# Stick-breaking attention: its softplus written as max(a, 0) + ln(1 + exp(-|a|)), with the absolute value on ScalarE

## The chip, the cores and the metric

The kernel runs on one core of a Trainium2 chip. A core has five engines that run at the same time, each through its own queue in order: TensorE (matrix products, PE in the profile), VectorE (DVE), ScalarE (ACT, functions of one input), GpSimd (POOL) and SyncE (SP, which here issues DMA transfers). They wait for each other only through semaphores. The metric is the device time of one execution in microseconds (us); lower is better. Of the kernel before three runs are known, and one more execution was profiled.

## The reference

One decoder block over 1024 tokens of width 1024: a state-space branch and an attention branch side by side, merged by gates, then a feed-forward network (FFN). The change concerns the attention branch, which has 8 heads of width 64 and weighs keys by stick breaking:

```python
z = jnp.einsum('bhqd,bhkd->bhqk', qb, kh) * scale
mask = key_pos < q_pos
log_not = jnp.where(mask, jax.nn.log_sigmoid(-z), 0.0)
suffix = lax.cumsum(log_not, axis=3, reverse=True) - log_not
weights = jnp.where(mask, jnp.exp(jax.nn.log_sigmoid(z) + suffix), 0.0)
return jnp.einsum('bhqk,bhkd->bhqd', weights, vh)
```

With softplus s(z) = ln(1 + exp(z)), `log_sigmoid(-z)` is -s(z) and `log_sigmoid(z)` is z - s(z). So a weight is the exponential of z minus the sum of s over this key and all later ones that the query sees, and s is needed once for each score.

## The kernel before

All products are f32 accurate: an operand is split into a high part in a reduced format and a low part (what is left), and three products of these parts are added. TensorE therefore issues three matmuls where one would do, and VectorE, ScalarE and GpSimd do the splits. The program runs through projections and the state-space branch, attention, the merge of the branches, the output projection, and the FFN.

**Attention** works on 40 units. A unit holds scores of two heads (one pair of heads shares the 128 partitions of q and k) for one or two blocks of 128 keys against up to 512 queries, with the keys on the partitions: a tile of 128 x 2 x w. For each of the 4 head pairs there are 10 units, 3 for the first 512 queries and 7 for the others, with the keys from the last to the first. Six of the 10 lie on the diagonal and take a mask; four of these are narrow (2 x 384), all other units are 2 x 512. The last four units of a pair have no mask.

A unit goes through three functions, and the loop in `attention` overlaps three units:

- `scores` (three units ahead): TensorE writes the scores into `z`, of which there is one PSUM buffer. They are copied to `a` (tile `wa`), with the mask added on VectorE (L871) or by a plain copy on ScalarE (L873). Then the softplus in tile `ws`: GpSimd takes min(a, 40) (L874), ScalarE Exp (L875) and Ln(1 + x) (L876), and VectorE max(a, that) (L877), which restores large values that the bound cut off. VectorE then splits it into `wh` (L878) and `wl` (L879). There are five buffers of `wa` and two each of `ws`, `wh` and `wl`.
- `sums`: TensorE multiplies the parts with a triangle of ones and adds the carried row of the units before, into `acc`, of which there is one PSUM buffer. ScalarE copies the total as the next carried row (L900), VectorE subtracts `acc` from `a` in two halves (L902) and takes the low part of the row (L904), and ScalarE applies the exponential (L905).
- `values`: TensorE multiplies the weights with V.

Between these, `fillers` gives TensorE matmuls of projections that are needed later (8 at each of two places in a unit), so that it has work while a unit's chain runs on the other engines. Their weights are split by L454, L456 and L457 on ScalarE, VectorE and GpSimd, and their results leave by copies (L841, L843, L846).

The matmuls of attention stay in the order in which the code issues them. The other engines' order is chosen when the program is built, by a scheduler with a model of the durations; each engine's list is then fixed. A change of durations or engines can therefore move instructions elsewhere too, as far as the first products of the FFN (`seven`, L1247), whose operands are formed and split on ScalarE and VectorE (L473, L475, L476).

The `acc` buffer sets the tightest loop: TensorE may start the next unit's sums only when L900, L902 and L904 have read it.

Of the kernel before, what the change touches and what calls it, by code (L numbers as in the profile page):

```python
# [12 lines left out]
AF = mybir.ActivationFunctionType  # L13
ALU = mybir.AluOpType
# [346 lines left out]
P = 128  # L361
KT = 8
MASKED = -1.0e30
EXACT = 40.0

AK, ARB = 1, 2

# [60 lines left out]
class Block:  # L428
# [421 lines left out]
    def scores(self, u, qk, work):  # L850


        nc = self.nc
        q, k = qk[u.hp]
        u.a, s = (work.tile([P, 2, 512], F32, name=t, bufs=b) for t, b in (("wa", WAB2), ("ws", WSB)))
        u.parts = [work.tile([P, 2, 512], F32R, name=t, bufs=WHB) for t in ("wh", "wl")]
        z = self.zp.tile([P, 2, 512], F32, name="z")
        u.segs, f, diag = [], 0, u.kbs[0] >= 4 * u.Q
        for kb in u.kbs:
            c = max(kb - 4 * u.Q, 0) * P  # L860
            w = 512 - c
            for x in range(2):
                h = slice(64 * x, 64 * x + 64)
                self.pinned(z[:, x, f:f + w], lhsT=k[h, P * kb:P * kb + P], rhs=q[h, 512 * u.Q + c:512 * u.Q + 512], start=True, stop=True)
            u.segs.append((kb, slice(f, f + w), slice(c, 512)))
            f += w
        u.f = f
        a, st, ht, lt, z = (t[:, :, 0:f] for t in (u.a, s, *u.parts, z))
        if diag:
            m = P * (2 - len(u.kbs))  # L870
            nc.vector.tensor_tensor(a, z, self.mask[:, m:m + f].unsqueeze(1).broadcast_to([P, 2, f]), ALU.add)  # L871
        else:
            nc.scalar.copy(a, z)  # L873
        nc.gpsimd.tensor_scalar(st, a, EXACT, None, ALU.min)  # L874
        nc.scalar.activation(st, st, AF.Exp)  # L875
        nc.scalar.activation(st, st, AF.Ln, bias=1.0)  # L876
        nc.vector.tensor_tensor(st, a, st, ALU.max)  # L877
        nc.vector.tensor_scalar(ht, st, 1.0, 0.0, ALU.mult, ALU.add)  # L878
        nc.vector.tensor_tensor(lt, st, ht.bitcast(F32), ALU.subtract)  # L879

# [650 lines left out]
```

## Time and profile before

| | |
|---|---|
| median of 3 runs | 1520.55 us (1516.18 to 1520.73) |
| profiled execution | 1517.3 us, of which the span of the profile 1515.5 |
| mean granted TensorE clock | 0.973 |

Busy time of the engines by stage, in us, from the windows of the profile:

| stage | span | length | TensorE | VectorE | ScalarE | GpSimd |
|---|---|---|---|---|---|---|
| projections, state-space branch, gates | 0 to 380 | 380 | 339.6 | 265.1 | 111.3 | 23.9 |
| attention | 380 to 677 | 297 | 289.1 | 247.6 | 171.9 | 145.0 |
| merge of the branches | 677 to 740 | 63 | 54.5 | 48.8 | 29.1 | 24.7 |
| output projection | 740 to 860 | 120 | 114.5 | 62.8 | 48.5 | 13.1 |
| FFN, gate and up | 860 to 1190 | 330 | 326.2 | 218.7 | 107.2 | 153.3 |
| FFN, down, last norm | 1190 to 1515 | 325 | 298.4 | 291.3 | 115.5 | 251.6 |

In the rows that follow, `L874` is line 874 of the kernel before; a group's row reads: line, engine, operation, tile written <- tiles read, shapes, count | busy us, mean ns of one | us that the engine sat idle before them, and what ended that. A row of the timeline reads: start us, duration us, engine, line, operation, tiles, shapes, count, and in brackets idle time before it. A window's row gives for each engine busy us and the number of instructions, then the granted clock, the share of the DMA engines and GB/s. A busy TensorE is not one at its peak, since matmuls overlap in the record.

### The profile page before, as it was taken

How to read it: one execution, taken by the hardware profiler on the slowest of the kernel's cores; microseconds unless marked ns; L12 is line 12 of the kernel's file. 1: busy time of each engine (PE TensorE's matmuls, PEld its weight loads, DVE VectorE, ACT ScalarE, POOL GpSimd, SP SyncE). 2: the span in 40 equal slices, each digit the busy share in tenths (PEclk: the TensorE clock that was granted, in tenths of full speed). 3: DMA queues.
4: the chain of work that ended last, by engine and by line, in shares of the span. 5: the costliest groups of instructions: out<-in, count | busy, mean ns of one | idle time of the engine just before them, and what ended most of it. 6: DMA issues, size and time to landing. Idle time of an engine off the chain costs nothing.

```text
span 1515.5 us, 18316 instructions
## 1 busy us (share of the span) xinstructions
PE 1422.3 (94%) x6706; PEld 1121.7 (74%) x6706; DVE 1134.3 (75%) x1523; ACT 583.5 (38%) x764; POOL 611.6 (40%) x306
## 2 busy tenths in 40 slices
PE   5898999997999999999799799999999998999995
PEld 3678888786666666658688588888888886888774
DVE  5779985455887988877625886666666769999998
ACT  3321122622474656564317533333333224343323
POOL 1000000102455555424300145444444468788795
PEclk9999999999999999999999899999999999999998
DMA  9555665388111112117523233333333246445312
GB/s 341 139 112 165 160 160 151 123 283 285 42 42 42 36 49 77 49 57 249 178 87 112 84 111 125 105 104 104 105 105 104 87 152 240 147 160 171 106 51 111
DMA packets 180410, 193.55 MB, mean 128 GB/s; under 512 B 28636, under 2 KB 130080, under 8 KB 180320
## 3 DMA queue, kind: packets, MB, share of 16 engines
q1 hardware_dynamic: 171184, 184.86, 38.8%
q10 hardware_dynamic: 8912, 7.48, 1.8%
q8 instruction: 53, 0.87, 0.2%
q14 instruction: 37, 0.30, 0.1%
q0 software_dynamic: 224, 0.05, 0.0%
HBM read 142.40 MB, written 48.76 MB: 126 GB/s over the span
## 4 chain that ended last, share of the span: by engine, by line
PE 40%; DVE 23%; issue 12%; DMA 10%; POOL 9%; ACT 5%; SPq 1%; DVEq 0%; POOLq 0%; ACTq 0%
PE tq L1247 10%; PE wo L1247 8%; PE wo L1128 5%; POOL ws L874 3%; DMA aw<-in_w_ada_dram 3%; PE gu L1247 3%; PE mm L809 2%; PE mm L643 2%; PE mx L809 2%; PE ga L735 1%; PE acc L809 1%; DVE acc L979 1%; POOL pb L1307 1%; PE mx L735 1%; DVE wa L902 1%
## 5 line engine op out<-in xcount | busy, mean ns | idle before, releaser
L874 POOL TENSOR_SCALAR ws<-wa 128x1024 f32<-128x1024 f32 (+1 forms) x40 | 109.3, 2733 | 117.6 <-DVE wa L871 59.0
L473 POOL TENSOR_TENSOR ws<-wb 128x1024 f32<-128x1024 f32 x26 | 64.2, 2471 | 191.1 <-DMA wb<-in_w_ffn_up_dram 88.6
L457 POOL TENSOR_TENSOR wl<-ws,wh 128x1024 fp32r<-128x1024 f32 x12 | 29.1, 2421 | 122.5 <-ACT wh L454 76.5
L294 POOL MEMSET tz<- 128x1024 f32 x4 | 3.8, 954 | 178.0 <-PE mm L643 95.2
L877 DVE TENSOR_TENSOR ws<-wa,ws 128x1024 f32<-128x1024 f32 (+1 forms) x40 | 46.8, 1169 | 35.6 <-ACT ws L876 35.2
L1300 POOL TENSOR_TENSOR pa<-pa,row 128x1024 f32<-128x1024 f32 x22 | 66.2, 3032 | 0.7 <-DMA pa<-in_w_ffn_down_dram 0.7
L875 ACT ACTIVATE ws<-ws 128x1024 f32<-128x1024 f32 (+1 forms) x40 | 38.9, 972 | 69.3 <-POOL ws L874 69.3
L473 POOL TENSOR_TENSOR wgs<-wb 128x1024 f32<-128x1024 f32 x14 | 35.6, 2540 | 73.3 <-DVE wgl L476 31.1
L1238 POOL TENSOR_TENSOR f<-f,f 128x512 f32<-128x512 f32 x30 | 49.0, 1660 | 26.1 <-DVE f L1228 17.6
L879 DVE TENSOR_TENSOR wl<-ws,wh 128x1024 fp32r<-128x1024 f32 (+1 forms) x40 | 55.6, 1390 | 1.1
L979 DVE SCALAR_TENSOR_TENSOR acc<-aw,cond,acc 128x512 f32<-128x512 f32 x56 | 44.0, 786 | 9.3 <-DMA aw<-in_w_ada_dram 8.5
L809 PE MATMUL z<-q,k 64*128 64x512 f32 (+3 forms) x192 | 42.6, 535 | 6.9 <-DVE gst L1062 6.9
L902 DVE TENSOR_TENSOR wa<-wa,acc 128x512 f32<-128x512 f32 (+1 forms) x80 | 46.7, 624 | 2.7 <-PE acc L809 1.8
L454 ACT CAST wh<-ws 128x1024 fp32r<-128x1024 f32 x24 | 25.0, 1048 | 59.7 <-PE wo L1128 34.9
L1227 ACT ACTIVATE f<-f 128x1024 f32<-128x1024 f32 x22 | 23.3, 1061 | 58.7 <-DVE f L1267 31.3
L1329 POOL TENSOR_TENSOR wb<-pa 128x512 f32<-128x512 f32 x23 | 39.6, 1731 | 15.6 <-DVE wxl L1327 5.5
L905 ACT ACTIVATE wa<-wa 128x1024 f32<-128x1024 f32 (+1 forms) x40 | 38.6, 964 | 13.8 <-DVE wa L902 13.8
L1238 POOL TENSOR_TENSOR f<-f 128x512 f32<-128x512 f32 x20 | 42.2, 2128 | 0.0
L1346 PE MATMUL wo<-f,f 128*128 128x512 f32 x132 | 40.6, 389 | 0.0
L476 DVE TENSOR_TENSOR wl<-ws,wh 128x1024 fp32r<-128x1024 f32 x20 | 28.3, 1415 | 15.9 <-ACT wh L475 15.9
L809 PE MATMUL mm<-wa,V 128*64 128x512 f32 (+3 forms) x192 | 39.8, 507 | 0.0
L876 ACT ACTIVATE ws<-ws 128x1024 f32<-128x1024 f32 (+1 forms) x40 | 38.7, 967 | 0.5
(839 smaller groups left out, 4720.5 us busy)
## 6 DMA issues: line engine op xcount, KB each, us to landing
aw<-in_w_ada_dram SPq DMA_DIRECT2D x64, 256.0 KB, 4.5
hD<-f SPq DMA_DIRECT2D x30, 512.0 KB, 2.8
ws<-in_w_in_dram SPq DMA_DIRECT2D x23, 512.0 KB, 5.2
wb<-in_w_ffn_gate_dram SPq DMA_DIRECT2D x44, 256.0 KB, 4.1
wb<-in_w_ffn_up_dram SPq DMA_DIRECT2D x44, 256.0 KB, 4.2
pa<-in_w_ffn_down_dram SPq DMA_DIRECT2D x22, 512.0 KB, 4.7
wb<-hD SPq DMA_DIRECT2D x40, 256.0 KB, 2.8
x<-in_x_dram SPq DMA_DIRECT2D x16, 512.0 KB, 7.4
```

Source lines behind the costliest of these rows:

```text
L473: (add or nc.gpsimd).tensor_tensor(st, a, b, op)
L809: return self.tc.keep_in_program_order(self.nc.tensor.matmul(*args, **kw))
L874: nc.gpsimd.tensor_scalar(st, a, EXACT, None, ALU.min)
L877: nc.vector.tensor_tensor(st, a, st, ALU.max)
L879: nc.vector.tensor_tensor(lt, st, ht.bitcast(F32), ALU.subtract)
L902: nc.vector.tensor_tensor(a[:, x, 0:f], a[:, x, 0:f], r[:, x, 0:f], ALU.subtract)
L979: nc.vector.scalar_tensor_tensor(acc, w[:, j], cj, acc, ALU.mult, ALU.add)
L1128: nc.tensor.matmul(ps, lhsT=mg[t // 4][k][:, a, P * (t % 4):P * (t % 4) + P], rhs=ws[k // 2][b][:, k % 2], start=(j == 0), stop=(j == 23))
L1238: nc.gpsimd.tensor_tensor(o, a, b, op)
L1247: self.nc.tensor.matmul(ps, lhsT=w[x][:, q, k], rhs=self.B[i](y, k), start=(j == 0), stop=(j == 11))
L1300: nc.gpsimd.tensor_tensor(w, w, g2, ALU.mult)
L1346: nc.tensor.matmul(ps, lhsT=o[x][:, P * t:P * t + P], rhs=o[y][:, R], start=(j == 0), stop=(j == 3 * np_ - 1))
```

## The change

The softplus is written as max(a, 0) + ln(1 + exp(-|a|)). The bound of 40 and its instruction on GpSimd go. ScalarE takes the absolute value, and Exp takes it with a scale of -1. The closing instruction on VectorE takes the larger of a and 0 and adds the logarithm (a scalar_tensor_tensor in place of a tensor_tensor).

```diff
 MASKED = -1.0e30
-EXACT = 40.0
...
-        nc.gpsimd.tensor_scalar(st, a, EXACT, None, ALU.min)
-        nc.scalar.activation(st, st, AF.Exp)
+        nc.scalar.activation(st, a, AF.Abs)
+        nc.scalar.activation(st, st, AF.Exp, scale=-1.0)
         nc.scalar.activation(st, st, AF.Ln, bias=1.0)
-        nc.vector.tensor_tensor(st, a, st, ALU.max)
+        nc.vector.scalar_tensor_tensor(st, a, 0.0, st, ALU.max, ALU.add)
         nc.vector.tensor_scalar(ht, st, 1.0, 0.0, ALU.mult, ALU.add)
         nc.vector.tensor_tensor(lt, st, ht.bitcast(F32), ALU.subtract)
```

Since one line goes, the changed kernel's lines below it are one less: its absolute value is L873, its Exp L874, its Ln L875, its closing instruction L876.

The first place where the order moves is ScalarE's list among the units without a mask. Before, from the copy of the eighth unit's scores (`wa_3865`, with `ws_3866`) to that of the ninth (`wa_3913`); `acc_3887` is the sixth unit's sum, `wa_3763` its exponential, `gst` a filler's result:

```order
L873 COPY wa_3865<-z_3869 128x1024
L900 CAST row1_3532<-acc_3887 1x1024
L846 COPY gst_3903<-mx_3835 128x512
L875 ACTIVATE ws_3866<-ws_3866 128x1024
L905 ACTIVATE wa_3763<-wa_3763 128x1024
L876 ACTIVATE ws_3866<-ws_3866 128x1024
L873 COPY wa_3913<-z_3917 128x1024
```

and of the changed kernel:

```order
L872 COPY wa_3865<-z_3869 128x1024
L873 ACTIVATE ws_3866<-wa_3865 128x1024
L874 ACTIVATE ws_3866<-ws_3866 128x1024
L899 CAST row1_3532<-acc_3887 1x1024
L875 ACTIVATE ws_3866<-ws_3866 128x1024
L845 COPY gst_3903<-mx_3835 128x512
L904 ACTIVATE wa_3763<-wa_3763 128x1024
L872 COPY wa_3913<-z_3917 128x1024
```

The copy, the absolute value and Exp of a unit now stand together ahead of the read of `acc`, and Ln behind it; before, both Exp and Ln stood behind it. On GpSimd only the fillers' weight splits stay in this stage. VectorE's list here keeps its order.

The second place is VectorE's list at the start of the FFN. `x1_7069` and `x1_7075` are low parts of the operand of one of the FFN's products, `wl_7127` the low part of a weight, `ft` the sums from which such operands are split. Before:

```order
L473 TENSOR_TENSOR ft_7070<-f0_6370,f0_6610 128x1024
L473 TENSOR_TENSOR ft_7076<-f0_6371,f0_6611 128x1024
L476 TENSOR_TENSOR wl_7127<-ws_7128,wh_7126 128x1024
L476 TENSOR_TENSOR x1_7069<-ft_7070,x1_7068 128x1024
L476 TENSOR_TENSOR x1_7075<-ft_7076,x1_7074 128x1024
L473 TENSOR_TENSOR ft_7116<-f1_6372,f1_6612 128x1024
```

and of the changed kernel:

```order
L472 TENSOR_TENSOR ft_7070<-f0_6370,f0_6610 128x1024
L472 TENSOR_TENSOR ft_7076<-f0_6371,f0_6611 128x1024
L475 TENSOR_TENSOR x1_7069<-ft_7070,x1_7068 128x1024
L475 TENSOR_TENSOR wl_7127<-ws_7128,wh_7126 128x1024
L472 TENSOR_TENSOR ft_7116<-f1_6372,f1_6612 128x1024
L475 TENSOR_TENSOR x1_7075<-ft_7076,x1_7074 128x1024
```

The operand's first low part has moved ahead of the weight's, its second behind it and behind another sum. TensorE's list follows: it takes the twelve matmuls of the first half of that operand in a row, then two other groups of twelve, and only then most of the second half.

## The prediction

> **What bounds the kernel now.** I read the page's busy shares first, then the attention stage by windows, then its groups by shape with the waits at the end of each row, then single stretches of the timeline. The change touches attention alone, 380 to 677 us of the span. In its middle (second row: length, then the engines in the order of the first, clock, DMA share, GB/s):
>
> ```profile
> PE 1422.3 (94%) x6706; PEld 1121.7 (74%) x6706; DVE 1134.3 (75%) x1523; ACT 583.5 (38%) x764; POOL 611.6 (40%) x306
> 400.00:655.00 255.00, 250.14 (x1139) 162.65 (x1139) 216.65 (x241) 148.95 (x174) 133.00 (x54) 1.00 0.15 47
> ```
>
> TensorE is busy for 250.14 of 255 us at a granted clock of 1.00, VectorE for 85%, ScalarE for 58%, GpSimd for 52%. Where attention is not disturbed, a unit takes what its matmuls take:
>
> ```profile
> 591.21 0.39 PE L809 MATMUL acc<-wh,upto 128*128 128x512 f32 x1
> 592.58 0.40 PE L809 MATMUL mx<-pa,wh 128*128 128x512 f32 x1
> 595.51 0.92 PE L809 MATMUL z<-q,k 64*128 64x384 f32 x4
> 596.36 0.73 PE L809 MATMUL mx<-pa,wh 128*128 128x512 f32 x2
> 598.30 0.40 PE L809 MATMUL acc<-wh,upto 128*128 128x512 f32 x1
> ```
>
> From one unit's first `acc` matmul to the next it is 598.30 - 591.21 = 7.09 us, without a gap. So 40 units cannot go below what TensorE issues, and all that a faster softplus can give back is TensorE's waits. They are the last figure of the first row here; the other rows are the prices used below.
>
> ```profile
> L809 PE MATMUL acc<-wh,upto 128*128 128x512 f32 x48 | 20.1, 418 | 7.7 <-DVE row L904 7.7
> L874 POOL TENSOR_SCALAR ws<-wa 128x1024 f32<-128x1024 f32 x24 | 71.7, 2986 | 81.9 <-ACT wa L873 53.4 <-DVE wa L871 28.5
> L874 POOL TENSOR_SCALAR ws<-wa 128x768 f32<-128x768 f32 x16 | 37.6, 2353 | 35.7 <-DVE wa L871 30.5 <-DMA nD<-gst 5.0
> L873 ACT COPY wa<-z 128x1024 f32<-128x1024 f32 x16 | 16.0, 998 | 0.0
> L875 ACT ACTIVATE ws<-ws 128x1024 f32<-128x1024 f32 x24 | 25.4, 1058 | 39.3 <-POOL ws L874 39.3
> L875 ACT ACTIVATE ws<-ws 128x768 f32<-128x768 f32 x16 | 13.5, 843 | 30.0 <-POOL ws L874 30.0
> L876 ACT ACTIVATE ws<-ws 128x1024 f32<-128x1024 f32 x24 | 25.3, 1052 | 0.3
> L900 ACT CAST row<-acc 1x1024 fp32r<-1x1024 f32 x16 | 16.1, 1004 | 11.5 <-PE acc L809 11.3
> L905 ACT ACTIVATE wa<-wa 128x1024 f32<-128x1024 f32 x24 | 25.2, 1049 | 3.0 <-DVE wa L902 3.0
> L877 DVE TENSOR_TENSOR ws<-wa,ws 128x1024 f32<-128x1024 f32 x24 | 30.8, 1285 | 22.4 <-ACT ws L876 22.2
> L878 DVE TENSOR_SCALAR wh<-ws 128x1024 fp32r<-128x1024 f32 x24 | 25.0, 1040 | 0.6
> L879 DVE TENSOR_TENSOR wl<-ws,wh 128x1024 fp32r<-128x1024 f32 x24 | 34.2, 1425 | 0.7
> L902 DVE TENSOR_TENSOR wa<-wa,acc 128x512 f32<-128x512 f32 x48 | 30.6, 678 | 2.7 <-PE acc L809 1.8 <-ACT row L900 0.9
> L904 DVE TENSOR_TENSOR row<-acc,row 1x1024 fp32r<-1x1024 f32 x16 | 19.4, 1214 | 0.5
> ```
>
> Seven times, 7.7 us in all, the next unit's `acc` waits until VectorE has read the single `acc` buffer (L902, L904). VectorE is late there because it runs in order, and its L877 waits 22.2 us in these units alone for Ln (L876), which waits for Exp (L875), which waited 39.3 us for the bound on GpSimd. The largest wait but one shows the queue:
>
> ```profile
> 613.50 1.23 DVE L877 TENSOR_TENSOR ws<-wa,ws 128x1024 f32<-128x1024 f32 x1 [1.10 <-ACT ws L876]
> 614.85 2.37 POOL L457 TENSOR_TENSOR wl<-ws,wh 128x1024 fp32r<-128x1024 f32 x1
> 615.24 2.54 DVE L878 TENSOR_SCALAR wh<-ws 128x1024 fp32r<-128x1024 f32 x1
> 618.95 1.01 DVE L902 TENSOR_TENSOR wa<-wa,acc 128x384 f32<-128x384 f32 x2
> 621.09 0.47 PE L809 MATMUL acc<-wh,upto 128*128 128x512 f32 x1 [1.95 <-DVE row L904]
> ```
>
> L902 starts some 5 us after its `acc` was complete, because a late L877 and a stretched L878 stand before it.
>
> **The change part by part.** *The bound goes.* Forty GpSimd instructions (109.3 us) leave the chain: per unit 2.99 us, or 2.35 for the narrow units. In their place ScalarE gets an absolute value. No row shows that function; the nearest are a copy and an Exp of the same width on ScalarE, 0.998 and 1.058 us, and I take 1.06 (0.843 narrow). The chain from scores to low part becomes 1.9 us shorter in a wide unit. ScalarE gains 24 x 1.058 + 16 x 0.843 = 38.9 us, some 36 of them in the window above: 149 + 36 = 185 of 255 us, 73%.
>
> *Does ScalarE still keep up?* A wide unit without a mask costs it 0.998 + 1.06 + 1.058 + 1.052 + 1.004 + 1.049 = 6.22 us of 7.09. Walk one turn of the new order from the end of `acc`: L900 to 1.00, Ln of a later unit to 2.05, the last exponential L905 to 3.10 (its two L902 end at 1.36). The next scores are complete 596.36 - 592.58 = 3.78 us after `acc`; copy, absolute value and Exp then end at 6.90, just before the next `acc` at 7.09. A cast or copy that falls in between (1.05 and 0.58 us; by the listing five and four times in these 16 units) delays L900, and the 0.7 us of idle before the scores takes that back in one or two units. `acc` is not held up before L900 is some 3.5 us late, since the next `acc` starts 5.72 us after this one ends and only L904 (1.21 us) has to follow L900. I allow 0.7 us for the worst of these coincidences.
>
> *The closing instruction on VectorE* becomes a scalar_tensor_tensor. Two rows bound it:
>
> ```profile
> L613 DVE SCALAR_TENSOR_TENSOR sqv<-x 128x1024 f32<-128x1024 f32 x4 | 4.9, 1224 | 5.0 <-DMA x<-in_x_dram 5.0
> L1371 DVE SCALAR_TENSOR_TENSOR pa<-pa,ss,gf 128x1024 f32<-128x1024 f32 x7 | 10.5, 1495 | 0.0
> ```
>
> Of the same width it took 1.224 us early in the program and 1.495 at its end; today's L877 takes 1.285. I take no change: between -0.06 and +0.21 us a unit, on an engine with more than 1 us to spare per wide unit (1.285 + 1.040 + 1.425 + 2 x 0.678 + 1.214 = 6.32 of 7.09). The Trainium skill, "Vector Engine (DVE) Microarchitecture Reference", section 7, says that this operation with two SBUF sources that are not bf16 runs at half throughput. By that the closing instruction would take about twice as long; L613 reads two f32 operands and shows nothing of it. What it would do here is the last rival.
>
> *VectorE also gets faster beside an idle GpSimd:*
>
> ```profile
> 651.35 2.91 POOL L874 TENSOR_SCALAR ws<-wa 128x1024 f32<-128x1024 f32 x1 [4.29 <-ACT wa L873]
> 651.66 1.41 DVE L878 TENSOR_SCALAR wh<-ws 128x1024 fp32r<-128x1024 f32 x1
> 658.07 0.70 DVE L878 TENSOR_SCALAR wh<-ws 128x1024 fp32r<-128x1024 f32 x1
> ```
>
> The same cast takes 1.41 us when it starts under the bound and 0.70 alone. With a mean of 1.040 that is 24 x 0.34 = 8 us of VectorE time; the weight splits that stay on GpSimd (L456, L457) can still stretch one, as at 615.24.
>
> *The waits, term by term.* The last two of the seven are at attention's end, where no scores are left and a unit has few matmuls to hide behind:
>
> ```profile
> 661.80 1.27 DVE L902 TENSOR_TENSOR wa<-wa,acc 128x512 f32<-128x512 f32 x2
> 663.10 1.21 DVE L904 TENSOR_TENSOR row<-acc,row 1x1024 fp32r<-1x1024 f32 x1
> 664.37 0.80 PE L809 MATMUL acc<-wh,upto 128*128 128x512 f32 x1 [2.24 <-DVE row L904]
> 664.96 0.63 PE L809 MATMUL acc<-wl,upto 128*128 128x512 f32 x1
> 665.39 0.63 PE L809 MATMUL acc<-wh,upto 128*128 128x512 f32 x1
> 671.02 0.50 PE L809 MATMUL acc<-wh,upto 128*128 128x512 f32 x1 [0.57 <-DVE row L904]
> ```
>
> The other five make 7.7 - 2.81 = 4.9 us. With a chain 1.9 us shorter and casts 0.34 shorter, VectorE reaches L902 when `acc` is complete in all but crowded units; I take 4.5 of the 4.9. At the end, L902 could start at 659.1 and starts at 661.80, 2.7 us late. In the new order VectorE still does five things before it (1.23 + 0.70 + 0.68 + 1.23 + 1.21 = 5.05 us after the L904 of the unit before, which ends 2.5 into its 7.09), so it is 0.5 late. The first wait nearly goes, and with it the slow matmuls behind it (0.43 us apart at 664.96 and 665.39, against 0.2275 in the steady stretch: eight of them, 1.6 us). The second grows, to about 1.5 us, as VectorE then has 8 us of work in a row: L902, L904, L877 to L879, L902, L904. From 659.1 the last `acc` ends after 10.2 us instead of 13.3: 3.1 us.
>
> *The order of the first FFN products moves* (the listing above):
>
> ```profile
> 870.06 1.22 DVE L476 TENSOR_TENSOR wl<-ws,wh 128x1024 fp32r<-128x1024 f32 x1
> 870.13 0.99 PE L1247 MATMUL tq<-x,wxh 128*128 128x512 f32 x2 [2.48 <-ACT x L475]
> 872.46 0.69 PE L1247 MATMUL tq<-x,wxh 128*128 128x512 f32 x1 [1.34 <-DVE x L476]
> ```
>
> The low part that TensorE waits for at 872.46 now comes before the weight's low part, 1.22 us sooner; the weight's is needed only over 40 matmuls (9 us) later. I take 1.1 us. The wait of 2.48 us before it is for ScalarE's cast and stays.
>
> Sum: 4.5 + 3.1 + 1.1 - 0.7 = 8.0 us. All that follows attention is fed by buffers that attention frees or by products of it, so the rest moves with it; I take nothing off for that. The profiled execution took 1517.3 us (span 1515.5 and 1.8 around it): 1509.3. The median of the runs shown stands 3.25 above it, so a median of runs should come to **1512.5 us**. From the unknown costs the sum has 5 to 12 us (a third of the middle waits staying and ScalarE costing 2 more; all of both gone and the FFN's slow matmuls too), so 1508.5 to 1515.5.
>
> **The rivals.** *Nothing to see* (1518.5): the waits are VectorE's own congestion. Its work before L902 stays, 6.3 us of 7.09 and more in units with a mask, and the stretched L878 at 615.24 was due to a weight split that stays. Then the middle keeps its 4.9, half of the end's 3.1 is lost to Ln, which now queues behind L900, and the FFN's 1.1 remains: about 2 us. Against it: 22.2 us of VectorE's idle time in the wide units is spent waiting for Ln.
>
> *ScalarE becomes the bound* (slower, 1531): the turn above fits with 0.2 us left. It decides once a unit costs ScalarE more than 7.09 us on average. A unit with a cast and a copy costs 6.22 + 1.05 + 0.58 = 7.85; if queueing made all 16 maskless units like that, they lose 0.76 each, 12 us, the waits stay, and 1.1 is gained. For it: the order puts L900, which frees `acc`, behind three instructions on the next scores. Against it: 73% busy and 0.7 us of slack in each turn.
>
> *The change isn't what it says:* if the absolute value lay in another function table, two reloads a unit of 1.28 us, the duration of each load in the profile, would add 100 us. The order of the changed kernel shows no added load.
>
> *Half throughput on VectorE* (1526): if L877 took twice the 1.224 us of L613, 24 x 1.2 + 16 x 1.0 = 45 us more on VectorE, 217 - 8 + 42 = 251 of 255 us; the masked units would be bound by it and the waits grow, by some 5 us net. This is the rule of the Trainium skill named above.
>
> **How the numbers follow.** Forecast 0.55, a larger gain 0.05, nothing to see 0.25, ScalarE 0.10, half throughput 0.02, the rest 0.03. Two results of this kernel within 0.3% (4.6 us) cannot be told apart, as its own runs spread by that. Faster beyond it, below 1516: 0.55 + 0.05 and a little of the rest, 0.62; the same 0.25; slower 0.13. The range for 8 in 10 is 1505 to 1521: it takes in the forecast, a larger gain and the no-change case, and leaves out ScalarE and half throughput.
>
> **What would show it.** In the new profile: no L874 on GpSimd; an absolute value of 1.0 to 1.1 us; the cast of the high part near 0.70 instead of 1.04; `acc` waiting for L904 for 1 to 2.5 us in all, mostly at the end; ScalarE at about 185 of the 255 us of the same stretch; attention shorter by 6 to 8 us. I am wrong if `acc` waits as before (VectorE's own congestion), if L900 starts more than 3 us after `acc` (ScalarE), or if attention ends sooner and the end does not.

## The result, and the profile after

The changed kernel takes 1511.95 us (median of 13 runs, 1505.21 to 1516.80); beside it the kernel before took 1520.04 (13 runs, 1516.18 to 1524.14). The ratio is 0.9947, 95% interval [0.9932, 0.9961]: 8.1 us faster. The forecast was 1512.5. The profiled execution took 1511.95 us, its span 1510.2.

The page's busy shares, and the same window of attention as before (length; busy time of TensorE, its weight loads, VectorE, ScalarE, GpSimd; clock, DMA share, GB/s):

```profile
PE 1416.4 (94%) x6706; PEld 1118.7 (74%) x6706; DVE 1127.3 (75%) x1523; ACT 622.1 (41%) x804; POOL 504.4 (33%) x266
400.00:655.00 255.00, 253.79 (x1165) 166.60 (x1164) 216.64 (x247) 188.79 (x216) 37.94 (x18) 1.00 0.15 47
```

ScalarE is at 188.8 us of the 255 (149 before; the forecast said 185), GpSimd fell from 133 to 38, VectorE stayed at 216.6. TensorE has 1.2 us of the window left.

The groups by shape that answer to those of before (busy us, mean ns of one | idle us ahead and what ended it):

```profile
L808 PE MATMUL acc<-wh,upto 128*128 128x512 f32 x48 | 19.0, 396 | 3.8 <-DVE row L903 3.8
L873 ACT ACTIVATE ws<-wa 128x1024 f32<-128x1024 f32 x24 | 25.5, 1062 | 16.0 <-DVE wa L870 15.5
L873 ACT ACTIVATE ws<-wa 128x768 f32<-128x768 f32 x16 | 13.6, 848 | 29.0 <-DVE wa L870 29.0
L876 DVE SCALAR_TENSOR_TENSOR ws<-wa,ws 128x1024 f32<-128x1024 f32 x24 | 30.2, 1258 | 1.8 <-ACT ws L875 1.1
L877 DVE TENSOR_SCALAR wh<-ws 128x1024 fp32r<-128x1024 f32 x24 | 18.7, 778 | 0.6
L878 DVE TENSOR_TENSOR wl<-ws,wh 128x1024 fp32r<-128x1024 f32 x24 | 36.7, 1530 | 0.6
L901 DVE TENSOR_TENSOR wa<-wa,acc 128x512 f32<-128x512 f32 x48 | 30.7, 680 | 12.5 <-ACT row L899 9.5 <-PE acc L808 3.1
L899 ACT CAST row<-acc 1x1024 fp32r<-1x1024 f32 x16 | 15.9, 993 | 2.4 <-PE acc L808 2.3
```

The wait for `acc` is 3.8 us in three pieces, where it was 7.7 in seven. VectorE no longer waits for Ln (1.8 us, before 22.4). It waits ahead of L901 instead: for `acc` itself, or for ScalarE's copy of its row, L899. It arrives early, as it should.

**Where the 8 us are.** From each unit's first `acc` matmul to the next, the changed kernel repeats one pattern of ten turns (6.87, 6.48, 7.00, 7.07, 6.69, 7.00, 7.31, 7.11, 7.09, 7.31 us). The exceptions are the first turn (5.87), one disturbed place in the middle (8.37 and 7.40 in place of 7.00 and 7.31) and the last two turns (5.71 and 5.68). The difference of each turn of before from the same turn of the changed kernel, worked out from the starts of those matmuls:

| part of the program | before minus after, us | forecast |
|---|---|---|
| attention, turns 1 to 37 without the next row: the five turns with a wait (they end at 427.7, 478.1, 506.8, 621.1, 643.3) and the ones beside them | 6.8 | 4.5 |
| one wait that is new, at 578.56, and the turn behind it | -1.5 | -0.7 |
| the last two turns | 1.9 | 3.1 |
| all 39 turns | 7.2 | 6.9 |
| from the first stalled matmul of the FFN to the end of the span | 1.9 in this pair, of which the order 0.8 (below) | 1.1 |

The sum comes out near the forecast (7.2 and 0.8 against 8.0), but the terms in attention do not: the middle gave more than forecast and the end less. In the single pair of profiles the whole span differs by 5.3 only. Attention began 3.1 us later in the profiled execution of the changed kernel, and two stretches that the table leaves out, from the first scores to the first `acc` and from the last `acc` to the FFN, were 0.3 us longer each; more of that in the last section.

The end of attention, on the timeline (start, length, engine, and in brackets the idle time ahead):

```profile
657.35 1.22 DVE L456 TENSOR_TENSOR wl<-ws,wh 128x1024 fp32r<-128x1024 f32 x1
658.00 0.98 ACT L899 CAST row<-acc 1x1024 fp32r<-1x1024 f32 x1
659.02 1.28 DVE L901 TENSOR_TENSOR wa<-wa,acc 128x512 f32<-128x512 f32 x2 [0.45 <-ACT row L899]
660.33 1.21 DVE L903 TENSOR_TENSOR row<-acc,row 1x1024 fp32r<-1x1024 f32 x1
661.60 0.50 PE L808 MATMUL acc<-wh,upto 128*128 128x512 f32 x1 [1.34 <-DVE row L903]
667.28 0.50 PE L808 MATMUL acc<-wh,upto 128*128 128x512 f32 x1 [1.21 <-DVE row L903]
```

`acc` was complete at about 657.3. L899 waits for ScalarE until 658.00, and L901 starts only when L899 has ended; then L901 and L903 follow. VectorE is free at 658.57 and stands idle for 0.45 us. The prediction had L901 run beside the row copy.

Half of the 1.9 us at the end hangs on the clock. The last turn took 6.65 us before and 5.68 after. The kernel before with only its closing instruction exchanged (below) has the order of before and nearly the same wait ahead of that turn (2.27 us, before 2.24), and its last turn took 5.69 us. The windows of that turn, in the profile of before and in that one:

```profile
664.37:671.02 6.65, 6.08 (x18) 3.95 (x18) 5.62 (x6) 2.21 (x3) 0.00 (x0) 0.74 0.06 22
662.67:668.36 5.69, 4.53 (x18) 2.75 (x19) 5.54 (x6) 2.21 (x3) 0.00 (x0) 1.00 0.07 27
```

The granted clock was 0.74 in the one and 1.00 in the other. With the clock alike the end gave 0.9 us.

The new wait in the middle:

```profile
570.44 3.25 POOL L456 TENSOR_TENSOR wgl<-wgs,wgh 128x1024 fp32r<-128x1024 f32 x1
571.46 2.78 DVE L877 TENSOR_SCALAR wh<-ws 128x1024 fp32r<-128x1024 f32 x1
575.90 1.27 DVE L901 TENSOR_TENSOR wa<-wa,acc 128x512 f32<-128x512 f32 x2
578.56 0.47 PE L808 MATMUL acc<-wh,upto 128*128 128x512 f32 x1 [1.21 <-DVE row L903]
```

A filler's weight split on GpSimd starts 1.0 us ahead of a cast, and the cast takes 2.78 us, against a mean of 0.778 in the group above. That is the kind of stretched cast that the prediction quoted at 615.24 of before; it has moved to another unit. That the split is what makes `acc` late here is read from the order in time; no run moved this split alone.

The start of the FFN:

```profile
866.67 1.22 DVE L475 TENSOR_TENSOR x<-ft,x 128x1024 fp32r<-128x1024 f32 x1
866.69 0.50 PE L1246 MATMUL tq<-x,wxh 128*128 128x512 f32 x1 [2.33 <-ACT x L474]
867.81 1.22 DVE L475 TENSOR_TENSOR wl<-ws,wh 128x1024 fp32r<-128x1024 f32 x1
867.95 0.50 PE L1246 MATMUL tq<-x,wxh 128*128 128x512 f32 x1 [0.76 <-DVE x L475]
```

The operand's low part runs ahead of the weight's, and the second stall comes 1.26 us after the first, before 2.33. But look at the clock (the column behind the engines) in the 7 us from that first matmul, before and after:

```profile
870.10:877.10 7.00, 5.63 (x15) 4.09 (x16) 7.00 (x6) 1.63 (x3) 3.22 (x1) 0.76 0.16 48
```

```profile
866.70:873.70 7.00, 6.24 (x26) 4.95 (x27) 7.00 (x5) 4.35 (x6) 3.26 (x1) 1.00 0.01 3
```

Before, it was granted 0.76 there, and eight matmuls in a row are 0.43 us apart instead of 0.2275; the changed kernel's profile has none of these. From the first FFN matmul to the end of the span it is 645.4 us before and 643.5 after, so clock and order are mixed in this pair. Two of the kernels below tell them apart. Both were granted 0.76 here; the first has the order of before (the bound put back into the chain), the second the changed order (the bound beside the chain, reading the score):

```profile
881.20:888.20 7.00, 5.65 (x16) 4.09 (x17) 7.00 (x5) 1.63 (x3) 3.23 (x1) 0.76 0.18 51
865.50:872.50 7.00, 6.22 (x19) 4.75 (x20) 7.00 (x6) 4.36 (x6) 3.25 (x1) 0.76 0.01 2
```

They take 646.0 and 645.2 us to the end. The 0.8 us show early and in every profile at that clock: one and the same matmul of TensorE's list starts 69.6 us behind the first FFN matmul in both profiles with the order of before, and 68.7 to 68.8 us behind it in all five with the changed order. In the three that were granted 1.00, all with the changed order, it starts at 67.1 to 67.2. So the order is worth 0.8 us at its place and the clock another 1.6.

Further on, the profiles part for other reasons. The profile of before is level with the first of the two kernels until some 530 us behind the first FFN matmul, and then gains 0.7, because it lacks a wait. That wait, in the first kernel and the second (who waits <- for whom: us in total, times, longest):

```profile
PE gu L1346 <- DVE x L1352: 0.5, 1, 0.5
PE gu L1348 <- DVE x L1354: 0.5, 1, 0.5
```

Ten of the twelve profiles have it at 0.5 us, one at 0.2, and the profile of before does not; why was not followed. Two others with the changed order at 0.76 differ in two earlier waits and take 643.7 and 644.2 us to the end. A third kernel with the changed order (without the bound, below) was granted 0.51 behind the stall:

```profile
868.90:875.90 7.00, 6.38 (x15) 4.72 (x16) 7.00 (x5) 4.28 (x6) 3.24 (x1) 0.51 0.02 3
```

It took 646.3 us. So the 1.9 us of this pair are 0.8 from the order and 1.7 from the clock (the changed kernel's 643.5 against 645.2 in the same order), less most of the 0.7 that the missing wait gave the profile of before.

### The profile page after: what moved, and what is told of

Read it like the earlier page. It is cut to its first block, busy times and chain, and to the rows that moved or that the text cites. A ratio compares the mean times of both kernels' runs of the same rounds, so it can differ in the third digit from the quotient of the medians.

```text
span 1510.2 us, 18260 instructions
## 1 busy us (share of the span) xinstructions
PE 1416.4 (94%) x6706; PEld 1118.7 (74%) x6706; DVE 1127.3 (75%) x1523; ACT 622.1 (41%) x804; POOL 504.4 (33%) x266
## 4 chain that ended last, share of the span: by engine, by line
PE 48%; DVE 23%; issue 9%; DMA 9%; POOL 6%; ACT 4%; SPq 0%; DVEq 0%; ACTq 0%; POOLq 0%
PE tq L1246 10%; PE wo L1246 8%; PE wo L1127 5%; PE mx L808 5%; PE mm L808 5%; PE gu L1246 3%; DMA aw<-in_w_ada_dram 3%; PE acc L808 2%; PE mm L642 2%; PE z L808 2%; DMA nD<-gst 1%; PE ga L734 1%; POOL pb L1306 1%; DVE acc L978 1%; PE mx L734 1%
## 5 line engine op out<-in xcount | busy, mean ns | idle before, releaser
L456 POOL TENSOR_TENSOR wl<-ws,wh 128x1024 fp32r<-128x1024 f32 x12 | 30.9, 2575 | 156.6 <-ACT wh L453 156.1
L901 DVE TENSOR_TENSOR wa<-wa,acc 128x512 f32<-128x512 f32 (+1 forms) x80 | 47.0, 628 | 34.0 <-ACT row L899 30.9
L873 ACT ACTIVATE ws<-wa 128x1024 f32<-128x1024 f32 (+1 forms) x40 | 39.1, 977 | 45.0 <-DVE wa L870 44.5
L876 DVE SCALAR_TENSOR_TENSOR ws<-wa,ws 128x1024 f32<-128x1024 f32 (+1 forms) x40 | 45.5, 1137 | 5.4 <-ACT ws L875 4.5
L455 POOL TENSOR_SCALAR wh<-ws 128x1024 fp32r<-128x1024 f32 x6 | 7.5, 1252 | 109.4 <-PE mx L808 39.3
L874 ACT ACTIVATE ws<-ws 128x1024 f32<-128x1024 f32 (+1 forms) x40 | 39.0, 974 | 1.1
L875 ACT ACTIVATE ws<-ws 128x1024 f32<-128x1024 f32 (+1 forms) x40 | 38.7, 968 | 0.4
```

Source lines behind the costliest of these rows:

```text
L876: nc.vector.scalar_tensor_tensor(st, a, 0.0, st, ALU.max, ALU.add)
L901: nc.vector.tensor_tensor(a[:, x, 0:f], a[:, x, 0:f], r[:, x, 0:f], ALU.subtract)
```

## The experiments

Ten kernels, in four groups: what the softplus's chain is worth, what GpSimd's company of VectorE is worth, how much room ScalarE has, and what is left at the end of attention. "Turns" is the sum of the 39 distances between the units' first `acc` matmuls: 277.3 us before, 270.1 after.

### The chain

**The kernel before without the bound, nothing in its place.** What is left out: Exp gets a scaled score, so the softplus is not the reference's.

```diff
-        nc.gpsimd.tensor_scalar(st, a, EXACT, None, ALU.min)
-        nc.scalar.activation(st, st, AF.Exp)
+        nc.scalar.activation(st, a, AF.Exp, scale=1.0 / 64.0)
```

> The kernel before without the bound: Exp reads the scores directly, scaled by 1/64 so that it stays finite (so the softplus of small scores is left out: the result is another function at the same cost). GpSimd leaves the chain and ScalarE gets nothing for it. If the chain through GpSimd made VectorE late (my theory), the ratio to before is 0.993 to 0.995 and acc waits for L904 2 to 4 us; what this is faster than the changed kernel is the price of the absolute value on ScalarE, 0 to 1.5 us. If the waits are VectorE's own congestion, the ratio is 0.998 to 1.000 and acc waits 6 to 8 us.

Measured: 1511.56 us, ratio 0.9948 [0.9931, 0.9965], turns 269.1. Its `acc` row, by shape:

```profile
L809 PE MATMUL acc<-wh,upto 128*128 128x512 f32 x48 | 19.1, 399 | 2.5 <-DVE row L903 2.4
```

Taking the bound out is the whole gain, and the absolute value put in its place costs 1.0 us in the turns and nothing that the runs can tell. So a chain that is shorter by another 1.06 us brings no more than this.

**The changed kernel with a bound on GpSimd put back into the chain** (a bound that no score reaches).

```diff
-        nc.scalar.activation(st, a, AF.Abs)
+        nc.gpsimd.tensor_scalar(st, a, 3.0e38, None, ALU.min)
+        nc.scalar.activation(st, st, AF.Abs)
```

> The changed kernel with a minimum (against 3e38, which changes no value) put back on GpSimd in front of the absolute value, so the chain holds both. If the chain decides, it is now 1.06 us longer than before: acc waits 9 to 16 us, ratio 1.001 to 1.006. If ScalarE's changed order or the new formula gave the gain, it is kept: ratio 0.995 to 0.998, acc waits under 5 us.

Measured: 1530.68 us, ratio 1.0082 [1.0064, 1.0101], turns 288.1: by the turns 18 us above the changed kernel and 10.8 above the one before. The time is more than expected; the waits for `acc`, 13.2 us in the two rows, are as expected.

```profile
L808 PE MATMUL acc<-wh,upto 128*128 128x512 f32 x48 | 20.4, 426 | 7.1 <-DVE row L904 6.1 <-DVE wh L878 1.0
L808 PE MATMUL acc<-wl,upto 128*128 128x512 f32 x48 | 20.4, 426 | 6.1 <-DVE wl L879 6.1
```

The second row says why. Besides waiting until `acc` is free, TensorE now waits 6.1 us for the low part itself. That wait is absent before and after: with both operations in the chain, the softplus is not ready when its unit's turn comes. The kernel before was near that edge already: what was 7.7 us of waiting with the bound alone is 13.2 with 1.06 us more. At the first FFN products this kernel has the order of before.

One thing moves together with the chain in all these kernels: the place of Exp in ScalarE's list. Compared with the kernel before, one Exp more stands ahead of 26 of the 32 row copies in the changed kernel, and of 31 in the kernel without the bound; in this one, of none. No kernel here changes the one without the other. What ScalarE waited for ahead of its 40 Exps in the profile of before speaks for the chain (us, times):

```profile
  POOL ws L874: 69.3, 35
```

At 35 of the 40 it stood idle until the bound was done. An earlier place of Exp in the list would not have started those sooner; a bound that is done sooner would. How much of the gain the new place brings behind that stays open.

**The kernel before with the closing instruction's new form alone.**

```diff
-        nc.vector.tensor_tensor(st, a, st, ALU.max)
+        nc.vector.scalar_tensor_tensor(st, a, 1.0, st, ALU.mult, ALU.max)
```

> The kernel before with its closing maximum as a scalar_tensor_tensor (times 1, then maximum), nothing else. By the rows of L613 and L1371 the closing instruction takes 1.25 to 1.35 us (1.285 before), ratio 0.999 to 1.001. By half throughput it takes 2.3 us or more and the ratio is 1.003 or more.

Measured: 1520.06 us, ratio 1.0008 [0.9991, 1.0025], turns 276.3.

```profile
L877 DVE SCALAR_TENSOR_TENSOR ws<-wa,ws 128x1024 f32<-128x1024 f32 x24 | 30.8, 1285 | 22.4 <-ACT ws L876 22.1
L809 PE MATMUL acc<-wh,upto 128*128 128x512 f32 x48 | 19.5, 407 | 8.3 <-DVE row L904 8.3
```

1285 ns, to the digit what the tensor_tensor of before took. The rival of half throughput does not hold here. The turns differ by 1.0 us from those of before, and all of it is the last turn, with the clock at 1.00 as shown above. The Trainium skill, "Vector Engine (DVE) Microarchitecture Reference", section 7, has this operation with two SBUF sources that are not bf16 at half throughput; the measurement disagrees, and the measurement decides.

### GpSimd beside VectorE

The change does two things at once: it shortens the chain, and it takes 109 us of GpSimd's work away from VectorE's side. Two kernels keep the chain short and put the work back, into a tile that nobody reads. TensorE's, VectorE's and ScalarE's orders are the changed kernel's in both.

**Forty idle bounds on an unrelated tile.**

```diff
+        nc.gpsimd.tensor_scalar(self.idle[:, :, 0:f], self.idle[:, :, 0:f], 40.0, None, ALU.min)
         nc.scalar.activation(st, a, AF.Abs)
```

> The changed kernel with the bound's instruction kept on GpSimd, of the same width, on a tile that nothing else uses: GpSimd is as busy as before, but not in the chain. VectorE's list and TensorE's are the changed kernel's. If the chain decides, most of the gain stays: ratio 0.995 to 0.997, acc waits 4 to 6 us, the cast of the high part back at 0.9 to 1.1 us. If what counted was GpSimd stretching VectorE's instructions, the gain goes: ratio 0.998 to 1.000, acc waits 7 us or more.

Measured: 1514.78 us, ratio 0.9968 [0.9953, 0.9983], turns 273.9. By itself this would say that company costs 3 us. But with no input to wait for, the forty did not spread over attention as before; they ran packed from 384 to 513 us:

```profile
420.00:513.00 93.00, 91.74 (x416) 59.39 (x414) 83.37 (x88) 72.77 (x84) 90.94 (x34) 1.00 0.13 40
```

GpSimd was busy for 90.94 of these 93 us; before it was busy for 49. The run did not test what it was meant to.

**The same, reading the score**, so that it runs where the old bound ran.

```diff
+        nc.gpsimd.tensor_scalar(self.idle[:, :, 0:f], a, 40.0, None, ALU.min)
         nc.scalar.activation(st, a, AF.Abs)
```

> The changed kernel, plus the bound of the kernel before computed on GpSimd again (same input, same shapes, same moments), but into a tile that nobody reads, so no chain waits for it. The order on TensorE, VectorE and ScalarE is the changed kernel's. Theory (the chain through GpSimd was the cost; GpSimd as a neighbour of VectorE costs a smaller part): the cast of the high part goes from 0.78 back to about 1.0 us, waits of acc rise from 4.7 to 6 to 8 us, attention grows by 1 to 4 us, time 1513 to 1516. Rival A (the relief of VectorE from GpSimd's company was the gain, not the chain): attention back at about 296, time about 1519. Rival B (the company costs nothing): 1512. One thing that is not off the chain: the copy or mask sum that next writes the input tile must wait for this GpSimd instruction, two units later.

Measured: 1512.44 us, ratio 0.9951 [0.9934, 0.9968], turns 270.2. The same stretch as above, and the groups:

```profile
420.00:513.00 93.00, 93.00 (x424) 61.15 (x423) 83.02 (x89) 74.00 (x84) 49.21 (x20) 1.00 0.14 42
L873 POOL TENSOR_SCALAR idle<-wa 128x1024 f32<-128x1024 f32 x24 | 69.7, 2902 | 73.4 <-ACT wa L872 36.1 <-DVE wa L870 25.1 <-PE mx L808 8.8
L877 DVE SCALAR_TENSOR_TENSOR ws<-wa,ws 128x1024 f32<-128x1024 f32 x24 | 32.3, 1346 | 1.0 <-ACT ws L876 0.3
L878 DVE TENSOR_SCALAR wh<-ws 128x1024 fp32r<-128x1024 f32 x24 | 23.8, 991 | 0.6
```

GpSimd does all of its old work at the old places. The cast is back to 0.99 us and the closing instruction up to 1.35. The time is the changed kernel's within the interval. So the relief of VectorE, real as it is (0.99 to 0.78 on the cast), is worth nothing in time; the chain, with the order of ScalarE that comes with it, is worth all of it. My own theory for this run, 1513 to 1516, was wrong; rival B had it. Put beside the second kernel above, forty such instructions cost 18 us of turns in the chain and none beside it.

### ScalarE's room

An added pass does more than fill ScalarE: the build orders ScalarE's list anew. With the pass in every unit, Exp is back behind the row copy, as before the change, at 29 of the 32 copies. With it in the units without a mask alone, Exp is back there in those units, and with it in the units with a mask, in most of those. So these three kernels measure the pass together with the order that it brings.

**The absolute value twice, in every unit.**

```diff
         nc.scalar.activation(st, a, AF.Abs)
+        nc.scalar.activation(st, st, AF.Abs)
```

> The changed kernel with the absolute value taken twice in a row on ScalarE: 7.28 us a unit without a mask, against the 7.09 of TensorE. If ScalarE becomes the bound beyond 7.09 (the working of the slower rival), these 16 units lose 0.2 to 0.75 us each, 3 to 12 us: ratio to before 0.997 to 1.003, and acc waits behind a late L899. If ScalarE has more room than I reckoned, the ratio stays at 0.994 to 0.996.

Measured: 1520.81 us, ratio 1.0014 [1.0000, 1.0028], turns 279.1. One more pass of 1.06 us a unit takes back the whole gain, with ScalarE at 209.7 of the 255 us from 400 to 655. The chain is still 0.87 us shorter than before in a wide unit (1.06 and 1.06 in place of 2.99), so its length alone does not explain the loss. The two kernels that follow put the pass into the one or the other kind of unit.

**Twice in the 16 units without a mask** (`if not diag:` ahead of the added line).

> The changed kernel with the absolute value computed twice, in the 16 units without a mask only (17 us more on ScalarE). Theory (ScalarE's room was what the slower rival of the prediction said: 6.22 of 7.09 us in a unit without mask, so 7.28 with this, past the point from which it decides): these units lose 0.2 to 0.5 us each, 3 to 7 us in all, time 1515 to 1519, nearly all that two absolute values in every unit cost (8.9). Rival (what cost 8.9 there was the longer chain in the units with a mask, where a late low part holds up VectorE): under 2 us here, time below 1514.

Measured: 1516.86 us median, ratio 0.9967 [0.9952, 0.9981], turns 272.4. Of the 2.3 us by the turns, 1.55 are in the last two, where the wait is 2.56 us instead of 1.34 and the granted clock in the last turn 0.72, and 0.8 in five turns of the middle.

**Twice in the 24 units with a mask** (`if diag:`).

> The changed kernel with the absolute value computed twice, in the 24 units with a mask only (22 us more on ScalarE). Theory (ScalarE is the bound only where it also copies the scores, in the units without mask): under 3 us, time 1512 to 1515. Rival (the chain in the masked units, by which VectorE gets its work): 5 to 9 us, time 1517 to 1521.

Measured: 1515.39 us median, ratio 0.9965 [0.9952, 0.9978], turns 273.3. The 3.2 us are in the middle: 1.26 in the turn that ends at 428.1, 1.02 at 627.1, the rest in small ones of up to 0.37.

The `acc` rows of the three, in this order:

```profile
L808 PE MATMUL acc<-wh,upto 128*128 128x512 f32 x48 | 20.0, 417 | 7.8 <-DVE row L904 7.4
L808 PE MATMUL acc<-wh,upto 128*128 128x512 f32 x48 | 19.3, 401 | 4.0 <-DVE row L905 4.0
L808 PE MATMUL acc<-wh,upto 128*128 128x512 f32 x48 | 19.3, 403 | 5.1 <-DVE row L905 5.0
```

Neither theory holds alone. Each kind of unit costs about 3 us by the ratios (2.3 and 3.2 by the turns), and the interval of each still touches that of the changed kernel; both together cost 10 by the ratios and 9.0 by the turns (1.0014 against 0.9947). So the two losses do not simply add up. That the room is shared, and that a delay which one kind leaves behind is absorbed by the other only while that one has room, would explain it, and so would the order; neither is shown. What the turns do exclude is that the units without a mask become bound at 7.09 us: with 7.28 us of ScalarE's work each, most of them kept their turn (the five that grew in the middle grew by 0.04 to 0.45).

### What is left at the end

**The first two later weights' low parts to GpSimd**, so that the L456 at 657.35 leaves VectorE's list.

```diff
-        ws = [self.w3(self.weight(src[:, :, 0:256]), 256)]
+        ws = [self.w3(self.weight(src[:, :, 0:256], lo_eng=nc.gpsimd), 256)]
```

(and the same for the next such weight)

> The changed kernel with the low parts of the first two weights of the merge (L457 on VectorE, 1.21 us each, in attention's last units) on GpSimd, which is idle there. VectorE then has 1.2 us less before the L902 of the last units. I expect the two waits at the end (3.1 us in the changed kernel) to fall to about 2, ratio to before 0.993 to 0.995; if those waits come from the chain of L902, L904 and L877 to L879 alone, nothing moves.

Measured: 1512.07 us, ratio 0.9956 [0.9942, 0.9970], turns 271.4. Nothing gained:

```profile
654.19 2.41 POOL L456 TENSOR_TENSOR wl<-ws,wh 128x1024 fp32r<-128x1024 f32 x1 [17.11 <-ACT wh L453]
654.29 3.39 DVE L878 TENSOR_TENSOR wl<-ws,wh 128x1024 fp32r<-128x1024 f32 x1
660.17 0.70 PE L808 MATMUL acc<-wh,upto 128*128 128x512 f32 x1 [1.85 <-DVE row L903]
```

The split that left VectorE ran beside VectorE's own low part and stretched it from 1.23 to 3.39 us. The wait at the end grew from 1.34 to 1.85. The one behind it fell from 1.21 to 0.43, but the granted clock in that turn was 0.74, and it took 6.49 us instead of 5.68.

**The subtraction ahead of the row copy**, since L901 starts only after L899.

```diff
+        for x in range(2):
+            nc.vector.tensor_tensor(a[:, x, 0:f], a[:, x, 0:f], r[:, x, 0:f], ALU.subtract)
         if kb:
             g.row = self.rows.tile()
             nc.scalar.copy(g.row[0:1, :, c], r[0:1, :, fs])
-        for x in range(2):
-            nc.vector.tensor_tensor(a[:, x, 0:f], a[:, x, 0:f], r[:, x, 0:f], ALU.subtract)
```

> The changed kernel with VectorE's subtraction of the sums placed ahead of ScalarE's copy of the sums' row. In the trace the subtraction starts only when the copy has ended, and the copy's chain (copy 0.99, subtraction 1.28, low part of the row 1.21) frees acc. With the two exchanged, VectorE can start when acc is complete and do the next unit's closing instruction during the copy. Theory (VectorE's idle microsecond per unit behind the copy is what keeps acc waiting at the end, 1.70 and 1.58 us): the end waits fall by about 0.8 us each, time 1510 to 1511.5. Rival A (the chain that frees acc has the same three links in either order): 1511.5 to 1512.5. Rival B (the last exponential and the row copy now queue behind other work on ScalarE, and the low part of the row behind VectorE's next unit): waits in the middle grow, time 1514 to 1520.

Measured: 1515.38 us, ratio 0.9974 [0.9962, 0.9986], turns 272.3: slower than the changed kernel by 4 us by the ratios. The groups, and the end on the timeline:

```profile
L898 DVE TENSOR_TENSOR wa<-wa,acc 128x512 f32<-128x512 f32 x48 | 30.8, 682 | 14.5 <-PE acc L808 14.4
L901 ACT CAST row<-acc 1x1024 fp32r<-1x1024 f32 x16 | 15.9, 997 | 9.4 <-DVE wa L898 9.2
656.36 1.29 DVE L898 TENSOR_TENSOR wa<-wa,acc 128x512 f32<-128x512 f32 x2
657.99 0.98 ACT L901 CAST row<-acc 1x1024 fp32r<-1x1024 f32 x1
658.12 1.23 DVE L876 SCALAR_TENSOR_TENSOR ws<-wa,ws 128x1024 f32<-128x1024 f32 x1 [0.47 <-ACT ws L875]
659.37 1.22 DVE L903 TENSOR_TENSOR row<-acc,row 1x1024 fp32r<-1x1024 f32 x1
660.64 0.50 PE L808 MATMUL acc<-wh,upto 128*128 128x512 f32 x1 [1.48 <-DVE row L903]
```

The first row shows the dependence turned round: the subtraction now waits for `acc` alone, and ScalarE's copy for the subtraction. At the end the wait is 1.48 instead of 1.34, since the row's low part now queues behind the next unit's closing instruction. In the middle two turns grew (553.6 by 0.59, 562.3 by 1.59). Rival B's mechanism, inside the range of its time. No version here beats the changed kernel.

## Why the prediction was right, step by step

**The mechanism held.** The forecast rested on one reading: TensorE waits for `acc` because VectorE is late, and VectorE is late because it queues behind a softplus that waits for GpSimd. Without the bound (first run) the gain is complete; with the bound's work kept but out of the chain (reading the score) it is complete too; with it in the chain it is lost and more. How the gain divides between the shorter chain and the new order of ScalarE's list is not shown, since no run separates the two.

**The middle: right in kind, undersized.** All five waits went. The forecast took 4.5 us of 4.9; the turns give 6.8, and the row of waits does not contain all of it: the five turns grew by 5.7 us for 4.9 of waits, the turns behind them by 0.8 (0.09 to 0.25 in the first turn behind each), and the second and third turn by 0.2. Against that stands 1.5 us for one new wait, where the forecast allowed 0.7, and named another cause: I charged it to ScalarE's casts and copies falling in between, and it came from a weight split on GpSimd that stretched a cast of VectorE's to 2.78 us.

**The end: oversized, and the step that failed is known.** "L902 could start at 659.1 and starts at 661.80, 2.7 us late", and in the new order "it is 0.5 late": this took it that L902 runs beside ScalarE's row copy; in the walk of ScalarE's turn I wrote "its two L902 end at 1.36", next to an L900 that ends at 1.00. L901 starts behind L899 (9.5 us of its idle time end with L899), and in no profile, before or after, does any of the 32 row copies overlap a subtraction of VectorE's. So `acc` is freed by three links in a row, 0.99 + 1.28 + 1.21 = 3.5 us, not by two. Before, ScalarE had a weight's cast to do first and ended L900 at 660.33 only, so L902 could not have started at 659.1 either. By the same sum the room that the walk gave L900, "some 3.5 us", is about 2.2. The waits are 1.34 and 1.21 us, where I had nearly none and 1.5. The end gave 1.9, not 3.1, and 1.0 of the 1.9 is the clock in the last turn: the prediction counted the slow matmuls behind the first wait as a part of that wait, while one of two profiles of this order has the wait without them. Net of the new wait the middle gave 1.5 us more than forecast and the end 1.2 less. That the two errors nearly cancel is luck; the total is closer than the working deserved.

**The FFN's order** moved as read: all profiles of kernels with the changed order show 1.26 us between the two stalls, those with the old order 2.33. Of the 1.1 us that the forecast took, 0.8 are there where the clock is alike, in two profiles of the one order against five of the other, so this term was nearly right. The pair of before and after hides it: the clock added 1.7 us, and the profile of before lacked a wait worth 0.7.

**ScalarE** is at 188.8 of 255 us against 185 forecast; absolute value 1.062 and 0.848 us against 1.06 and 0.843. That the rival "ScalarE becomes the bound" would not come was right. Its condition was wrong: it was put at 7.09 us a unit, and in units without a mask alone. What the runs show is a smaller room: at an average of 74% in the window, one further microsecond a unit, with the order that it brings, takes the whole gain away.

**VectorE's relief** was given as 8 us of its time. The casts gave 6.3 (24 x 0.262), the low parts took 2.5 back (1.425 to 1.530), and in the window VectorE is as busy as before (216.65 and 216.64), for 247 instructions in place of 241. The run with the idle bounds that read the score shows that it would not have mattered.

**The other rivals.** "Nothing to see" said that VectorE's own work holds `acc` up whatever the chain does. VectorE is as busy in the window as it was, and the five waits of the middle went nevertheless. A reload of function tables is not in the profile: it has nine table loads, as many as before, and absolute value, Exp and Ln stand 1.06 us behind one another. The closing instruction cost 1.258 us, inside its bounds.

## What to carry over

When an engine that works in order is late, look along its queue for the instruction that waits longest, and follow that wait to the engine it comes from: here 22 us of waiting for Ln were a GpSimd instruction two steps earlier, and replacing that one by an instruction on an engine that had room was worth the 8 us. A busy share of 74% does not say how much more an engine takes; add one instruction and measure it, and look at what the build then does to the order. When two profiles differ, compare the granted clock of the stretch before the order of the instructions gets the credit or the blame: a third and a fourth profile told them apart here. And write down for each pair of readers of one buffer whether they run together or one after the other: the trace showed it before the change, in a row that I had quoted and passed over.

## What the runs showed that was not expected

- In the stretches shown, a tensor_tensor on GpSimd slowed VectorE by more than the old bound did: a cast went from 0.70 to 2.78 us, a low part from 1.23 to 3.39, while the bound of before brought a cast from 0.70 to 1.41. The two instructions work on different tiles.
- Two readers of one `acc`, on ScalarE and VectorE, run one after the other in whichever order the program has them (9.5 us of waiting for L899 in the changed kernel, 9.2 us for L898 with the two exchanged). Whether the chip needs that or only the program's synchronization makes it so was not tried.
- The granted clock right behind the stall at the first FFN matmul differs from profile to profile, 1.00, 0.76 or 0.51 over 7 us, worth 0 to 2.8 us. A longer stall does not mean a lower clock: 0.51 stands behind the shortest (2.01 and 2.06 us), 1.00 behind 2.33 to 2.55, 0.76 behind 2.48 to 3.00. The Trainium skill, "TensorE: Matmul & The Clock Gate", part 1, says that the clock is set by a window of activity that runs freely. By that a like stall can catch the window at another phase; the spread agrees with that, and no run here shows the window itself.
- In the last turn of attention a longer wait does go with a lower clock, though not always. Where the wait ahead of it was 1.85 us or more, the granted clock was 0.72 to 0.74 in five of six profiles and 1.00 in the sixth; where it was 1.58 or less, it was 1.00 in all six.
- The program ahead of attention, the same in all twelve kernels, is not equally long in every execution. The rows of the first scores, before and after (least, median and longest duration, then first and last start):

```profile
L809 PE MATMUL z<-q,k x8: 418/605/631, 380.3 to 381.3; 64*128 64x128 f32 x4, 64*128 64x256 f32 x4
L808 PE MATMUL z<-q,k x8: 417/604/631, 383.4 to 384.4; 64*128 64x128 f32 x4, 64*128 64x256 f32 x4
```

Over the twelve profiles the first start lies between 379.1 and 385.1 us, nearly as much as the effect to be measured. Two single spans of this kernel cannot be told apart by less than some 6 us; its undisturbed turns in attention repeat to 0.02 us.
